# Seven block products in place of eight for the first layer's pooled gate, on a renormalised input, in a two-layer trunk

## The chip, the cores and the metric

The kernel runs on one core of a Trainium2 chip. The metric is the time of one execution in microseconds of the device, taken as the median of several runs. Five engines work in parallel, each through its own queue of instructions: TensorE (PE, matmuls; PEld is its loading of weights), VectorE (DVE), ScalarE (ACT), GpSimd (POOL) and SyncE (SP, which here only issues DMAs). DMAs are issued by SP, ACT and POOL.

## The reference, cut to what matters

A residual stream of T = 528 tokens (16 meta tokens and 512 others) by 1024 passes through two layers. Each layer is

```python
h = rmsnorm(h_res, norm_gain[l])
proj = h @ w_in[l]
u_pool, z_pool, c_q, c_kv, k_rope, z_mla, g_pool, g_mla = jnp.split(proj, IN_SPLIT_POINTS, axis=-1)
y_pool = (pool_mix(u_pool, ...) * jax.nn.silu(z_pool)) @ pool_w_up[l]
o_mla = mla(c_q, c_kv, k_rope, pos, ...)          # 8 heads, causal, rotary
y_mla = (o_mla * jax.nn.silu(z_mla)) @ mla_w_up[l]
merged = jax.nn.sigmoid(g_pool) * y_pool + jax.nn.sigmoid(g_mla) * y_mla
h_res = h_res + merged @ w_out[l]
```

and the output is the stream without the meta tokens. `g_pool` and `g_mla` are 1024 wide each: `h` (528 x 1024) times a 1024 x 1024 block of `w_in`. All is float32.

## The kernel before, in words

The stream lies transposed in SBUF: 8 row blocks of 128 features by the tokens (`xb`). A product in float32 is made of three: weights and input are each split into a high part in a shorter format and the rest (`split`, and `wload` for weights: ScalarE copies `hi`, VectorE subtracts to get `lo`), and `mm3` (L188, L191, L192) multiplies hi by hi, hi by lo and lo by hi into one PSUM bank. Weights come from DRAM in pieces of 128 x 512 (256 KB), three buffers deep, split as they come, four pieces ahead.

Nearly all matrix products of a layer stand in one list, `plan` (made by `register`, in the order in which it adds them: ckv, cq, u, k, v, zp, y, the queries qr and qn, pu, zm, the gates gp and gm, mu, o). `stream` walks through it. The rest of the program draws from the stream: `upto(name)` runs it up to a product, `fill_now(ns)` for so many nanoseconds of planned products. A planned product of three matmuls counts 3 n/2.4 ns for n columns, and `clk` is the sum of what has been drawn; it is a planner's clock, not the chip's. `after(ns, fn)` puts a step on the list until `clk` has grown by so much. The final order on each engine is set by a scheduler within these bounds.

In the attention of a layer (`head`, `pv`) the eight heads' own matmuls alternate with gaps (`gap`, four for each head), which draw the gates' products from the stream: `FILL` nanoseconds of them each, 2950 in the first layer and 2700 in the second, up to gm5 (`RESERVE`). A head's chain is: scores on TensorE, the maximum with the mask on VectorE (L886), the exponential on ScalarE (L893), scaling by the inverse sum on POOL (L900), transposes on TensorE (L957), a split, and the product with the values (L962, L963).

The two layers form their gates differently. In the first layer the input is x times the gain, not yet divided by the norm (`split_h`), all 528 tokens, in two halves of 264 columns. `ev_gp`, `ev_gm` and the `ev_silu` of zm multiply each result by the inverse norm `self.inv` (L716, L1038, L553) on VectorE; then comes Tanh on ScalarE. In the second layer (`self.last`) only 512 tokens are computed, and at the end of `qk_stats` the input is normalised and split anew (`renorm`, L576; row blocks 0 to 3 are fetched from DRAM as `xb` has been overwritten there). The gate gp of two neighbouring output tiles is a product of a 2 x 2 block of weights with a 2 x 2 block of input (two halves of K, two halves of the tokens); `fast` forms its four results from seven block products in place of eight, with sums of weights and of inputs. The input's sums and differences are made by `mixed` in the gaps (eight calls, four subtractions and three splits alternating), the weights' sums by DMA alone: `weight_sums` copies one block from DRAM to DRAM by SP (L350) and adds another to it by POOL (L353), eight transfers for each pair of tiles. Each is held behind a matmul that lies 14 us (copy) or 4 us (addition) back in planned time. The gates gm0 to gm5 of the second layer are stored in DRAM by ACT (L1047), from the slots `tc` and `ts` of the rotary tables, and fetched again before mu (`gates_again`). The last four columns of `wout` use the same seven products in both layers (`out_pairs`, `blend`).

## Time and profile before

| what | value |
|---|---|
| time, median of 3 runs | 782.66 us (782.34 to 786.49) |
| the profiled execution's own time | 781.06 us |
| its span | 779.3 us |
| granted TensorE clock | 1.0 throughout |
| TensorE busy | 772.7 us, 5469 matmuls |
| VectorE, ScalarE, POOL busy | 570.4, 445.9, 232.1 us |
| read from DRAM, written | 100.18 MB, 22.62 MB |
| first layer's attention | about 180 to 340 us |
| second layer's attention | about 580 to 700 us |

The profile is of one execution. Busy times overlap between engines. A matmul's own duration holds its way through the array and overlaps the next one's; the distance between the starts of two is what one costs. In the rows, "a<-b,c" is what an instruction writes and reads by the program's names, `L184` a line of the kernel, which can be that of a helper, and the number behind the bar the busy time, the mean of one in nanoseconds, then the idle time of the engine ahead of it and what ended it. In the rows of one tile or line, three numbers with slashes are the shortest, the median and the longest duration in nanoseconds. Rows that end in "x139, 256.0 KB, 3.0" are DMA issues with the median microseconds to landing.

### The profile page before, as it was taken

The numbers are of one execution on the slowest core, as the hardware profiler recorded it, in microseconds if no ns is written. First come the engines' busy times: TensorE is split into PE (matmuls) and PEld (weight loads), VectorE is DVE, ScalarE is ACT, GpSimd is POOL, SyncE is SP. The second block draws the span as 40 slices with busy tenths as digits, with TensorE's granted clock in tenths as the row PEclk, the third lists the DMA queues.
The fourth block names the chain that finished last, engine by engine and source line by source line (L and its number), as shares of the span: only waits on it lengthen the run. The fifth ranks groups of instructions, "written<-read, shape, count | busy, mean of one in ns | idle before, by whom it ended". The sixth has DMA issues, their size and how long they took to land.

```text
span 779.3 us, 15360 instructions
## 1 busy us (share of the span) xinstructions
PE 772.7 (99%) x5469; PEld 711.3 (91%) x5469; DVE 570.4 (73%) x1332; ACT 445.9 (57%) x1022; POOL 232.1 (30%) x303
## 2 busy tenths in 40 slices
PE   8999999999999999999999999999999999999998
PEld 8999899999999999999998898888788999988887
DVE  5848787546778876589764577865897888874984
ACT  7645655645566665645564346556657766664552
POOL 1024514103335333211330136112006625440213
PEclk9999999999999999999999999999999999999999
DMA  6243457765746465565662523435557666662655
GB/s 245 82 96 89 114 170 159 181 170 144 156 109 165 116 140 120 156 166 176 169 172 82 100 85 101 133 97 175 137 132 168 172 184 161 176 208 90 204 155 143
DMA packets 66189, 112.92 MB, mean 145 GB/s; under 512 B 10800, under 2 KB 16816, under 8 KB 66112
## 3 DMA queue, kind: packets, MB, share of 16 engines
q1 hardware_dynamic: 56208, 92.18, 39.8%
q0 software_dynamic: 8896, 17.92, 12.7%
q10 hardware_dynamic: 1008, 1.84, 0.7%
q8 instruction: 43, 0.70, 0.4%
q14 instruction: 34, 0.28, 0.1%
HBM read 100.18 MB, written 22.62 MB: 158 GB/s over the span
## 4 chain that ended last, share of the span: by engine, by line
PE 90%; DMA 4%; DVE 3%; ACT 2%; issue 1%; POOL 1%; SPq 0%; ACTq 0%; DVEq 0%
PE mm L188 26%; PE mm L192 25%; PE mm L191 25%; DMA raw<-win 2%; PE S L191 2%; PE S L192 2%; PE S L188 2%; PE mm L957 2%; PE o L963 1%; PE o L962 1%; PE S L500 1%; DVE wlo L184 1%; ACT whi L183 1%; DMA raw<-wqb 1%; PE mm L402 1%
## 5 line engine op out<-in xcount | busy, mean ns | idle before, releaser
L188 PE MATMUL mm<-hh,whi 128*128 128x264 f32 (+2 forms) x992 | 306.5, 311 | 0.9 <-ACT whi L183 0.8
L192 PE MATMUL mm<-hh,wlo 128*128 128x264 f32 (+2 forms) x992 | 304.2, 309 | 0.1
L191 PE MATMUL mm<-hl,whi 128*128 128x264 f32 (+2 forms) x992 | 304.1, 308 | 0.0
L184 DVE TENSOR_TENSOR wlo<-raw,whi 128x512 fp32r<-128x512 f32 (+2 forms) x261 | 182.5, 703 | 104.6 <-ACT whi L183 100.5
L183 ACT ACTIVATE whi<-raw 128x512 fp32r<-128x512 f32 (+2 forms) x261 | 156.6, 603 | 175.1 <-PE mm L191 106.6
L188 PEld LDWEIGHTS mm<-hh,whi 128*128 128x128 f32 x992 | 186.2, 188 | 11.9 <-ACT whi L183 1.1
L191 PEld LDWEIGHTS mm<-hl,whi 128*128 128x128 f32 x992 | 186.8, 188 | 8.8
L192 PEld LDWEIGHTS mm<-hh,wlo 128*128 128x128 f32 x992 | 185.8, 188 | 9.0 <-DVE wlo L184 0.7
L900 POOL TENSOR_SCALAR pa<-pa,rs 128x272 f32<-128x272 f32 (+1 forms) x32 | 33.2, 1036 | 103.3 <-DVE rs L919 63.9
L900 POOL TENSOR_SCALAR cq<-cq,rs 128x400 f32<-128x400 f32 (+1 forms) x32 | 51.1, 1597 | 0.0
L188 PE MATMUL mm<-cq,whi 128*128 128x264 f32 (+2 forms) x140 | 44.0, 314 | 0.6 <-ACT tmp L702 0.6
L191 PE MATMUL mm<-cq,whi 128*128 128x264 f32 (+2 forms) x140 | 43.5, 312 | 0.0
L192 PE MATMUL mm<-cq,wlo 128*128 128x264 f32 (+2 forms) x140 | 43.4, 312 | 0.0
L886 DVE CUSTOM_DVE_ANT_0 S<-S,maskw,nqs 128x272 f32<-128x272 f32 (+4 forms) x80 | 38.6, 498 | 5.3 <-PE S L192 5.0
L703 POOL TENSOR_TENSOR racc<-racc,tmp 128x264 f32<-128x264 f32 (+1 forms) x15 | 14.2, 949 | 87.2 <-ACT tmp L702 87.1
L298 DVE TENSOR_TENSOR tl<-mm,th 128x512 fp32r<-128x512 f32 (+1 forms) x64 | 30.0, 483 | 8.0 <-ACT th L297 6.3
L188 PE MATMUL mm<-u,whi 128*128 128x264 f32 (+1 forms) x108 | 35.2, 326 | 0.0
L192 PE MATMUL mm<-u,wlo 128*128 128x264 f32 (+1 forms) x108 | 34.8, 322 | 0.0
L353 POOL DMA_DIRECT2D wsum<-wout x8 | 7.0, 873 | 91.8 <-PE mm L192 87.1
L297 ACT ACTIVATE th<-mm 128x512 fp32r<-128x512 f32 (+1 forms) x64 | 26.2, 433 | 10.3 <-PE mm L957 9.8
L893 ACT ACTIVATE cq<-S,bia 128x400 f32<-128x400 f32 (+2 forms) x48 | 24.4, 513 | 13.2 <-DVE bia L931 8.5
L191 PE MATMUL mm<-kn,whi 128*128 128x264 f32 (+1 forms) x96 | 30.6, 320 | 0.0
(334 smaller groups left out, 1672.6 us busy)
## 6 DMA issues: line engine op xcount, KB each, us to landing
raw<-win SPq DMA_DIRECT2D x139, 256.0 KB, 3.0
raw<-wout SPq DMA_DIRECT2D x22, 256.0 KB, 3.6
bc<-kdr SPq DMA_DIRECT2D x16, 264.0 KB, 4.8
wsum<-wout SPq DMA_DIRECT2D x16, 256.0 KB, 4.0
raw<-wpu SPq DMA_DIRECT2D x16, 256.0 KB, 3.2
wsumgp<-win SPq DMA_DIRECT2D x16, 256.0 KB, 3.4
raw<-wmu SPq DMA_DIRECT2D x16, 256.0 KB, 2.6
raw<-wsumgp SPq DMA_DIRECT2D x16, 256.0 KB, 3.6
```

Source lines behind the costliest of these rows:

```text
L183: act.activation(hi[:, :n], raw[:, :n], AF.Copy)
L184: dve.tensor_sub(lo[:, :n], raw[:, :n], hi[:, :n].bitcast(F32))
L188: first = pe.matmul(out, wh, xh, start=start, stop=False, skip_group_check=more)
L191: pe.matmul(out, wh, xl, start=False, stop=False, skip_group_check=more)
L192: newest[0] = pe.matmul(out, wl, xh, start=False, stop=stop, skip_group_check=more)
L297: act.activation(hi[:, a:b], src, AF.Copy)
L298: dve.tensor_sub(lo[:, a:b], src, hi[:, a:b].bitcast(F32))
L703: self.acc_last = gp.tensor_add(self.acc[:, a:b], self.acc[:, a:b], t[:, :b - a])
L886: dve.tensor_tensor_reduce(out=sv, in0=sv, in1=mask, scale=nqs[:, i, h:h + 1], scalar=3e38, op0=ALU.add, op1=ALU.min, accum_out=bia[:, c:c ...
L893: act.activation(pv, sv, AF.Exp, scale=-1.0, bias=bia[:, i:i + 1], accum_out=rs[:, c:c + 1])
L900: gp.tensor_scalar(pt[i], pt[i], rs[:, i:i + 1], None, op0=ALU.mult)
L957: pe.transpose(tr[:, P * (i - j):P * (i - j + 1)], pt[i][:, NM + P * j:NM + P * (j + 1)], ident)
```

## The change

The first layer's path for the gates becomes that of the second. At the end of `qk_stats` both layers normalise and split the input anew; in the first layer blocks 0 to 3 are fetched from the kernel's input and the tokens are all 528, halves of 264. `ev_gp` and `ev_gm` go, `ev_zm` and `ev_gate` serve both layers, and gp is made by `fast` in both, its four pairs placed between the gm tiles. The constant halves of the tokens become `self.halves()`. Since gm uses the slots of the rotary tables, these are stored to DRAM after they are made (`kept`, by POOL) and fetched at the start of the second layer (`tables_again`, by SP). There are now sums of weights for gp of both layers: those for gp of the first, for `wout` of the first and for three of the four pairs of the second are started from the end of ckv1, one transfer every 3300 ns of planned time (`SUMS`), before 3850 from `k_factors` on; the fourth pair and `wout` of the second follow in the second layer, also every 3300 in place of 4500. `FILL` of the first layer is 2800.

```diff
-FILL = (2950.0, 2700.0)
+FILL = (2800.0, 2700.0)
+SUMS = 3300.0
...
+        for d, t in zip(kept, tab):
+            gp.dma_start(d, t)
+
+    def tables_again():
+        tab[:] = slot("tc")[:, :T], slot("ts")[:, :T]
+        for d, t in zip(kept, tab):
+            sp.dma_start(t, d)
...
-    wsum = {... for n, k in (("gp", 4), (0, 2), (1, 2))}
-    gate = dp.tile([P, 6, SEQ], F32, name="gate")
+    wsum = {... for n, k in (("gp0", 4), ("gp1", 4), (0, 2), (1, 2))}
+    gate = [dp.tile([P, 6, T], F32, name=f"gate{l}") for l in range(DEPTH)]
...
         def renorm(self, k):
-            f, (hh, hl), x = f[:, NM:T], self.hs[k], xb[:, k, NM:T]
+            x0 = self.x0
+            f, (hh, hl), x = f[:, x0:T], self.hs[k], xb[:, k, x0:T]
             if k < 4:
-                sp.dma_start(f, scr[:, k, :])
+                sp.dma_start(f, scr[:, k, :] if self.last else xT[:, k, :])
...
         def mixed(self, i):
-            if k > 3 or not self.last:
+            if k > 3:
                 return
+            a, b, c = self.halves()
+            n = b - a
...
-            if self.last:
-                start = clk[0]
-                for i, k in enumerate((4, 5, 6, 7, 0, 1, 2, 3)):
-                    self.renorm(k)
-                    fill_to(start + 1500 * (i + 1))
-            else:
-                fill_now(9500)
+            start = clk[0]
+            for i, k in enumerate((4, 5, 6, 7, 0, 1, 2, 3)):
+                self.renorm(k)
+                fill_to(start + 1500 * (i + 1))
...
         def ev_gate(self, m):
             def ev(ps, a, b):
-                self.gms[m] = slot(f"cq{m}" if m > 5 else "ts" if m % 2 else "tc")
+                if a == self.x0:
+                    self.gms[m] = slot(f"cq{m}" if m > 5 else "ts" if m % 2 else "tc")
                 act.activation(self.gms[m][:, a:b], ps, AF.Tanh, scale=0.5)
                 if m < 6:
-                    act.dma_start(gate[:, m, :], self.gms[m][:, a:b])
+                    act.dma_start(gate[self.l][:, m, a:b], self.gms[m][:, a:b])
...
-            if self.last:
-                for e in ("gm0", "gm1", "gp0", "gm2", "gp1", "gm3", "gp2", "gm4", "gp3", "gm5", "gm6", "gm7"):
...
-            else:
-                for m in range(8):
-                    add(f"gp{m}", wi(MT_GP + m), D, evac=self.ev_gp(m), xs=hs, segs=XS)
-                for m in range(8):
-                    add(f"gm{m}", wi(MT_GM + m), D, evac=self.ev_gm(m), xs=hs, segs=XS)
+            for e in ("gm0", "gm1", "gp0", "gm2", "gp1", "gm3", "gp2", "gm4", "gp3", "gm5", "gm6", "gm7"):
+                m = int(e[2])
+                if e[:2] == "gp":
+                    self.fast(e, wi(MT_GP + 2 * m), wi(MT_GP + 2 * m + 1), m, self.got_gp)
+                else:
+                    add(e, wi(MT_GM + m), D, evac=self.ev_gate(m), xs=hs, segs=XS)
...
         def go(self, nxt):
             up("ckv1")
...
+            if l == 0:
+                wg = [[win[l_, MT_GP + m] for m in range(8)] for l_ in range(DEPTH)]
+                sums = [*weight_sums("gp0", wg[0]), *weight_sums(0, [wout[0, m] for m in OUT]),
+                        *weight_sums("gp1", wg[1], range(3))]
+                for i, fn in enumerate(sums):
+                    after(SUMS * (i + 1), fn)
+            else:
+                tables_again()
...
-            if l == 0:
-                sums = [*weight_sums(0, [wout[0, m] for m in OUT]), *weight_sums("gp", [win[1, MT_GP + m] for m in range(8)])]
-                for i, fn in enumerate(sums):
-                    after(3850 * (i + 1), fn)
...
-            if l == 0:
-                fill_now(2600)
             kq = self.prep(0)
             if l == 1:
-                for i, fn in enumerate(weight_sums(1, [wout[1, m] for m in OUT])):
-                    after(4500 * (i + 1), fn)
+                sums = [*weight_sums("gp1", [win[1, MT_GP + m] for m in range(8)], (3,)),
+                        *weight_sums(1, [wout[1, m] for m in OUT])]
+                for i, fn in enumerate(sums):
+                    after(SUMS * (i + 1), fn)
...
-            if self.last:
-                self.gates_again()
+            self.gates_again()
```

More of the change, by code (lines that the diff above doesn't have):

```diff
@@ L353, in add @@
             behind(gp.dma_start(d, src[1], accum_op=ALU.add), earlier(4000))
-        for u in range(len(w) // 2):
+        for u in units or range(len(w) // 2):
             for fn, i in ((copy, 0), (copy, 2), (add, 0), (copy, 1), (add, 2), (add, 1), (copy, 3), (add, 3)):
@@ L571, in renorm @@
             f = self.f[k] = slot("sv", bufs=2) if k % 4 == 3 else slot(f"cq{k}")
[L572 removed]
+            x0 = self.x0
+            f, (hh, hl), x = f[:, x0:T], self.hs[k], xb[:, k, x0:T]
             if k < 4:
[L574 removed]
+                sp.dma_start(f, scr[:, k, :] if self.last else xT[:, k, :])
                 x = f
[L576 removed]
+            behind(dve.scalar_tensor_tensor(out=f, in0=x, scalar=self.g(G_H + k), in1=self.inv[:, x0:T],
                                             op0=ALU.mult, op1=ALU.mult), newest[0])
[L578 removed]
+            split(hh, hl, f, x0, T)
         def mixed(self, i):
             k, s = divmod(i, 2)
[L582 removed]
+            if k > 3:
                 return
+            a, b, c = self.halves()
+            n = b - a
             u, w = self.f[k], self.f[k + 4]
@@ L595, in mixed @@
             th, tl = (slot(f"cq{(3, 0, 1, 2)[k] + j}", F32R) for j in (0, 4))
-            t3h, t3l, t4h, t4l = (t[:, :N2] for t in self.half[4 * k:4 * k + 4])
+            t3h, t3l, t4h, t4l = (t[:, :n] for t in self.half[4 * k:4 * k + 4])
             split(th, tl, u[:, a:c], a, c)
             for h_, l_, v in ((t3h, t3l, w[:, b:c]), (t4h, t4l, w[:, a:b])):
-                split(h_, l_, v, 0, N2)
+                split(h_, l_, v, 0, n)
             self.tt[k] = {6: (th[:, a:b], tl[:, a:b]), 5: (th[:, b:c], tl[:, b:c]), 7: (t3h, t3l), 4: (t4h, t4l)}
@@ L603, in fast @@
             order = (1, 6, 7, 5, 2, 4, 3)
-            s = wsum["gp"][u]
+            s = wsum[f"gp{self.l}"][u]
+            lo, mid, hi = self.halves()
+            n = mid - lo
+            A, B = (lo, mid), (mid, hi)
             src = {1: a[:, 0:512], 2: a[:, 512:1024], 4: b[:, 512:1024], 5: s[:, 0, :], 6: s[:, 1, :], 7: s[:, 2, :],
@@ L710, in ev @@
                 act.activation(self.am[m][:, a:b], ps, AF.Copy)
-            return ev
-        def ev_gp(self, m):
-            def ev(ps, a, b):
-                t = tmp()
-                dve.tensor_mul(t[:, :b - a], ps, self.inv[:, a:b])
-                act.activation(t[:, :b - a], t[:, :b - a], AF.Tanh, scale=0.5)
-                dve.scalar_tensor_tensor(out=self.am[m][:, a:b], in0=t[:, :b - a], scalar=1.0,
-                                         in1=self.am[m][:, a:b], op0=ALU.add, op1=ALU.mult)
             return ev
@@ L1052, in gates_again @@
                 self.gms[m] = slot(f"cq{m}")
-                sp.dma_start(self.gms[m][:, NM:T], gate[:, m, :])
+                sp.dma_start(self.gms[m][:, self.x0:T], gate[self.l][:, m, self.x0:T])
         def ev_mu(self, m):
@@ L1330, in go @@
             up("gm6")
-            if self.last:
-                self.gates_again()
+            self.gates_again()
             up("gm7")
```

63 lines of the change are left out of this document (23 added, 40 removed).

## The prediction

> **What bounds the kernel now.** I read the page first (engine shares and the chain that ended last), then stretches of the span by engine, then single rows.
>
> ```profile
> span 779.3 us, 15360 instructions
> PE 772.7 (99%) x5469; PEld 711.3 (91%) x5469; DVE 570.4 (73%) x1332; ACT 445.9 (57%) x1022; POOL 232.1 (30%) x303
> ...
> PE 90%; DMA 4%; DVE 3%; ACT 2%; issue 1%; POOL 1%; SPq 0%; ACTq 0%; DVEq 0%
> ```
>
> TensorE is busy 99% of the span and makes 90% of the chain. So a matmul taken out is worth its own time, as long as the engines that feed it keep ahead. The stretches show whether they do; columns are stretch, length, then busy time of each engine, clock, DMA share.
>
> ```profile
> core 0: us, PE busy (x) PEld busy (x) DVE busy (x) ACT busy (x) POOL busy (x), PEclk, DMA share, GB/s
> 20.00:92.00 72.00, 72.00 (x606) 67.02 (x605) 51.44 (x118) 39.05 (x88) 25.12 (x26) 1.00 0.34 95
> 92.00:127.00 35.00, 34.38 (x277) 33.99 (x276) 25.82 (x70) 18.53 (x41) 6.96 (x13) 1.00 0.62 157
> 127.00:180.00 53.00, 53.00 (x446) 51.31 (x445) 29.80 (x69) 29.79 (x74) 11.50 (x14) 1.00 0.68 168
> 180.00:340.00 160.00, 160.00 (x1300) 158.16 (x1299) 118.37 (x318) 93.53 (x243) 58.09 (x79) 1.00 0.58 140
> 550.00:580.00 30.00, 30.00 (x138) 24.25 (x138) 29.05 (x70) 19.75 (x39) 0.89 (x1) 1.00 0.44 118
> 580.00:700.00 120.00, 119.55 (x782) 108.49 (x781) 100.62 (x264) 81.26 (x213) 57.99 (x71) 1.00 0.67 182
> 155.00:180.00 25.00, 25.00 (x215) 23.68 (x208) 11.11 (x35) 11.06 (x27) 1.65 (x2) 1.00 0.64 160
> ```
>
> The attention of the first layer, with its gates in the gaps, is 180 to 340; that of the second, where seven products are already in use, is 580 to 700. The second is the model for what the first becomes: there TensorE idles 120 - 119.55 = 0.45 us, with VectorE busy 100.62/120 = 84% and ScalarE 81.26/120 = 68%. The first has 74% and 58% and no idle TensorE. The renormalising of the second layer lies in 550 to 580, that of the first would come into 155 to 180.
>
> **The products removed.** Eight gate tiles take 8 x 2 halves x 8 blocks of K x 3 = 384 matmuls of 264 columns. Seven products for each of four pairs take 4 x 7 x 4 x 3 = 336. So 48 fall away. Their price is the distance between starts, as a single matmul's duration overlaps the next one's:
>
> ```profile
> 127.75 0.28 PE L191 MATMUL mm<-cq,whi 128*128 128x264 f32 x1
> ...
> 137.99 0.28 PE L191 MATMUL mm<-cq,whi 128*128 128x264 f32 x1
> ```
>
> Those are the first and the last of 85 rows in a row, all of 264 columns: (137.99 - 127.75)/84 = 0.122 us. 48 x 0.122 = **-5.85 us**, all of it on the path.
>
> **The vector work of the gates.** These rows price it.
>
> ```profile
> L716 DVE TENSOR_TENSOR tmp<-mm,rinv 128x264 f32<-128x264 f32 x16 | 6.8, 428 | 3.2 <-PE mm L192 3.1
> L1038 DVE TENSOR_TENSOR cq<-mm,rinv 128x264 f32<-128x264 f32 x16 | 6.9, 430 | 6.2 <-PE mm L192 6.0
> L553 DVE SCALAR_TENSOR_TENSOR u<-mm,rinv 128x264 f32<-128x264 f32 x8 | 3.4, 431 | 0.7 <-PE mm L192 0.6
> L184 DVE TENSOR_TENSOR wlo<-raw,whi 128x512 fp32r<-128x512 f32 x233 | 168.5, 725 | 95.7 <-ACT whi L183 93.8
> L298 DVE TENSOR_TENSOR hl<-cq,hh 128x528 fp32r<-128x528 f32 x8 | 5.6, 702 | 0.0
> L298 DVE TENSOR_TENSOR u<-cq,cq 128x264 fp32r<-128x264 f32 x8 | 3.2, 426 | 0.0
> L183 ACT ACTIVATE whi<-raw 128x512 fp32r<-128x512 f32 x233 | 146.1, 630 | 164.6 <-PE mm L191 104.2 <-DMA raw<-win 24.2 <-issue 8.6
> L297 ACT ACTIVATE hh<-cq 128x528 fp32r<-128x528 f32 x8 | 5.1, 640 | 4.3 <-DVE cq L1063 4.3
> L297 ACT ACTIVATE cq<-cq 128x264 fp32r<-128x264 f32 x8 | 3.0, 415 | 0.2
> ```
>
> Away go the multiplications by the inverse norm at the gates and at zm: 16 x 0.428 + 16 x 0.430 + 8 x 0.431 = 17.2 us of VectorE. Added in `mixed` are 16 subtractions of a half (0.43), and for each of four k one split of a full row and two of a half: VectorE 16 x 0.43 + 4 x (0.70 + 2 x 0.43) = 13.1, ScalarE 4 x (0.64 + 2 x 0.42) = 5.9. `fast` adds five combinations of a half for each pair, 20 x 0.43 = 8.6 of VectorE, and four copies on ScalarE (1.7). The weights come in 4 x 7 = 28 pieces in place of 16, since each piece now feeds 12 matmuls, not 24: 12 more splits, VectorE 12 x 0.725 = 8.7, ScalarE 12 x 0.63 = 7.6. Net VectorE 13.1 + 8.6 + 8.7 - 17.2 = +13.2, ScalarE +15.2. In a stretch of 160 - 5.85 = 154 us VectorE comes to 131.6/154 = 85%, ScalarE to 108.7/154 = 71%: the level of the second layer. Taking that layer's idle rate, 0.45 x 154/120 = **+0.6 us**. The bounds are -0.3 (shorter eviction of zm and the gates) and +3.4 (eight `mixed` calls each keeping TensorE back 0.42 us, one half-row operation).
>
> The gates gm keep their Tanh, their storing to DRAM moves 12 issues onto ScalarE's queue, and the reload of six rows waits on SyncE for the `cq` rows of the last pair, with the mu weights behind it. Between that pair and the first use lie two gate tiles, 96 matmuls x 0.122 = 11.7 us, and mu0. I take 0; without that cover the price is one landing.
>
> **Renormalising.** It replaces 9.5 us of filler by eight steps of 1.5 us, and the 2.6 us before the first head go, so the first head comes at the same point (12.1 against 12.0 us of planned products).
>
> ```profile
> L576 DVE SCALAR_TENSOR_TENSOR cq<-xb,gn,rinv x3: 729/750/753, 549.0 to 553.3; 128x512 f32<-128x512 f32 x3
> ...
> L576 DVE SCALAR_TENSOR_TENSOR sv<-sv,gn,rinv x1: 733/733/733, 563.6 to 563.6; 128x512 f32<-128x512 f32 x1
> 178.44 0.28 PE L188 MATMUL mm<-hh,whi 128*128 128x264 f32 x1
> ```
>
> The cost is 8 x (0.75 x 528/512 + 0.70) = 11.8 us of VectorE and 8 x 0.64 = 5.1 of ScalarE, into a stretch (155 to 180) where VectorE has 13.9 and ScalarE 13.9 us free. The second layer needs from 549.0 to about 565, 16 us. Here from 156 that ends near 172, and the first product that reads the new input, zm0, starts at 178.44. The pu products (192 x 0.122 = 23.4 us) hide it: **0**. Were VectorE 10 us later, TensorE would wait some 4 us.
>
> **Sums of weights.** There are 96 transfers in place of 64, half of them copies on SyncE, half additions that POOL issues; 72 of them belong to the first layer, one every 3.3 us of planned products from the end of ckv1 (2.6 us ahead of the sums of the norm, L402 at 24.26, so about 21 us), in place of 48 from 91 us, one every 3.85.
>
> ```profile
> L353 POOL DMA_DIRECT2D wsum<-wout x8: 812/860/1046, 110.7 to 648.2; - x8
> L353 POOL DMA_DIRECT2D wsumgp<-wsumgp x8: 833/884/897, 198.8 to 344.8; - x8
> L350 SPq DMA_DIRECT2D wsum<-wout x16: 496/519/1087, 91.3 to 647.1; - x16
> 24.26 2.36 PE mm L402 x40
> raw<-win SPq DMA_DIRECT2D x139, 256.0 KB, 3.0
> 106.53 4.88 DMA raw<-win
> PE mm L188 <- ACT tmp L702: 0.6, 1, 0.6
> PE mm L957 <- POOL pa L900: 0.2, 1, 0.2
> 586.96 0.82 POOL L353 DMA_DIRECT2D wsum<-wout  x1 [8.83 <-PE mm L192]
> 587.56 1.40 POOL L900 TENSOR_SCALAR pa<-pa,rs 128x272 f32<-128x272 f32 x1
> L900 POOL TENSOR_SCALAR pa<-pa,rs x32: 632/960/2813, 180.7 to 689.4; 128x272 f32<-128x272 f32 x16, 128x144 f32<-128x144 f32 x16
> ```
>
> The first 20 to 92 us ran at a DMA share of 0.34 and will run near 0.6. The nearest rows are the three stretches at 0.58 to 0.68: 0.62 us of idle TensorE in 35 + 53 + 160 = 248 us, all of it at 126, where a weight piece took 4.88 us to land against a median of 3.0. At that rate 72 us cost 0.2, and at the rate of 92 to 127 alone 1.3. Below nothing: the wait at 126 may vanish (-0.6), since the order of transfers there changes. I take **+0.3**. Behind the copies on SyncE queue weight pieces; behind the additions on POOL queue the sums of squares, the rotary products, the window sums and, in the attention, the softmax scaling. The row at 586.96 shows the last: an addition ahead of a scaling, and TensorE waits 0.2 us. In the second layer's attention 12 additions replace 8: **+0.1**, at most 4 x 0.9 = 3.6 if each cost its whole issue. The Trainium skill, page "SBUF — State Buffer", section "SBUF: two separate sides" (its warning box on POOL's DMAs, with figures in the section after it), says the reverse of this cheapness: descriptors of POOL's DMAs can't be written while certain VectorE operations hold the shared port, so that a transfer of 0.62 us alone took 3.1 us. Here the longest issue is 1.05 us while VectorE is 74 to 84% busy, so no such lock shows in the issues; it keeps a small chance below.
>
> All first-layer sums end near 72 x 3.3 = 238 us of planned products after 21 us, about where the last one ends now (345 us); the pairs' own sums, first in the list, are 32 x 3.3 = 106 us in, well ahead of the first pair. The rotary tables' store and reload and the small edits at meta queries: 0, in queues with nothing urgent behind. FILL falls by 0.15 us in each of 32 gaps, 4.8 us, against 48 x 0.11 = 5.3 us of planned products less: the filler lasts as long as before.
>
> **Sum.** -5.85 + 0.6 + 0.3 + 0.1 = -4.85 us. The profiled run took 781.06 us (span 779.3 and 1.8 around it); 776.2 after. The median of the runs, 782.66, is 1.6 us above it, so **777.8**. 0.5% of the median, about what a measurement of this kernel tells from no change, is 3.9 us: faster means under 778.75.
>
> **Rivals.** First, half is given back: weight pieces arrive late in the first 130 us, each time as at 126. Five more such waits of 0.62 cost 3.1 us: 780.9. For it: VectorE and ScalarE have little room at 92 to 127 (74% and 53%) and three pieces in a row arrive late there. Against: 127 to 180 has the highest DMA share and no idle time. Chance 0.17.
>
> Second, slower: the first layer's head chain gets behind VectorE's new queue. Eight times a `mixed` call puts 1.6 to 1.7 us of work (four subtractions, or three splits) before a head's maximum, and TensorE waits for it. All eight cost 8 x 1.6 = 12.8, 790.6; with six it is 787.4; it decides from three on (4.85/1.6), where nothing is left. Against: the second layer makes the same eight calls and idles 0.45 us altogether. For: this layer's gap is shorter than before and has the meta queries as well. Chance 0.11.
>
> Third, slower, by POOL's queue: additions hold POOL and the softmax scaling behind them is late by as much as the longest scaling row lies over the median, 2.81 - 0.96 = 1.85 us. Some seven more additions fall into attention (18.7 in place of 16 in the first layer, 12 in place of 8 in the second): 7 x 1.85 = 13.0, less 4.85, gives 790.8; from three on nothing is left. It is the case by the port rule above; the issues of 0.8 to 1.05 us speak against. Chance 0.04.
>
> That fewer products aren't what comes out (the stream runs dry before the last head and TensorE waits there) would give about 782.7; filler and gaps shrink alike. Chance 0.03.
>
> **Numbers.** The forecast has 0.65 and covers 776.2 to 778.7. Faster than that by losing the wait at 126 and a quiet run (0.3 below the median): 775.8, the low end. The high end takes in the first rival and no gain at all: 783.0; beyond lie the second and third. Faster by over 0.5%: 0.65 + 0.02 of the first rival = 0.67; within 0.5%: 0.15 + 0.03 = 0.18; slower: 0.15.
>
> **What would show it.** TensorE's count falls by 48 to about 5421 and its busy time by 5 to 6 us; 180 to 335 has VectorE at 84 to 86% and TensorE idle under 1 us; zm0 starts near 178 with no wait for `hl`; the stretch 20 to 92 has a DMA share near 0.6 and TensorE busy over 99%. I am wrong if TensorE waits on ScalarE's `whi` or VectorE's `wlo` before 130 us (first rival), on VectorE's bias or `hl` between 155 and 340 (second), on POOL's `pa` (third).

## The result

The changed kernel takes 804.26 us (median of 6 runs, 798.37 to 806.32) against 782.8 before: a ratio of 1.0262, 95% interval 1.0238 to 1.0286. It is slower by 2.6%, where I had forecast 0.6% faster.

First the page of the kernel after, the same lines as shown of before.

```profile
span 803.9 us, 15499 instructions
...
PE 779.4 (97%) x5421; PEld 714.3 (89%) x5421; DVE 587.5 (73%) x1368; ACT 460.3 (57%) x1058; POOL 246.9 (31%) x321
...
PE 84%; DMA 6%; DVE 5%; ACT 2%; issue 1%; POOL 0%; SPq 0%; ACTq 0%; DVEq 0%; POOLq 0%
```

The 48 matmuls are gone (5469 to 5421). TensorE's idle time has grown from 779.3 - 772.7 = 6.6 to 803.9 - 779.4 = 24.5 us, and its busy time has grown by 6.7 although it has less to do. DMA has gone from 4% to 6% of the chain, VectorE from 3% to 5%. TensorE's waits, longest first (who waited for whom, us in total, times, longest):

```profile
PE mm L189 <- ACT whi L184: 7.0, 3, 4.0
PE o L962 <- ACT th L298: 4.7, 1, 4.7
PE S L189 <- ACT sv L1131: 2.3, 1, 2.3
PE mm L957 <- POOL pa L900: 1.9, 2, 1.7
```

The first is a weight piece that isn't there. The second looks like attention's own work on ScalarE; ScalarE's order of time ahead of it shows what it is:

```profile
323.99 0.63 ACT L298 ACTIVATE q<-tmp 128x512 fp32r<-128x512 f32 x1
330.11 0.63 ACT L184 ACTIVATE whi<-raw 128x512 fp32r<-128x512 f32 x1 [5.49 <-DMA raw<-win]
330.64 0.58 ACT L298 ACTIVATE th<-mm 128x512 fp32r<-128x512 f32 x1
```

ScalarE stands 5.49 us before the split of a weight piece that hasn't landed, and attention's split `th` is queued behind it. The chain of work has that piece; after the start in us stands its time from issue to landing:

```profile
321.12 8.89 DMA raw<-win
```

That is 8.89 us against the median of 3.0 before. SyncE's order of time around it shows what it shares the engines with:

```profile
320.11 0.90 SPq L1043 DMA_DIRECT2D cq<-gate  x2
321.12 0.37 SPq L116 DMA_DIRECT2D raw<-win  x1
321.53 1.39 SPq L1043 DMA_DIRECT2D cq<-gate  x3
```

The piece is issued between five rows of stored gates, 264 KB each, which the change makes the first layer fetch again, and one addition of a sum is issued by POOL at 320.79. So the longest wait has the reload beside it and not the sums alone. More on this stands below, with the runs that leave sums out.

The wait at 60 us came in another way. Its chain holds a store of the inverse norms (`ndr`), and only then the weight piece:

```profile
41.58 10.68 DMA ndr<-ny
...
53.24 6.58 DMA raw<-wkb
```

SyncE may fetch the norms only when their store has landed, and stands before the two fetches for 8.1 us, in the kernel before for 7.8; the weight pieces are queued behind them in both. What differs is the landing of the piece: 6.58 us, against a median of 2.0 for the pieces of `wkb` before, and it meets a stream that has just run short.

Each long wait has an aftermath. In these short stretches the last three columns are the granted clock, the DMA share and GB/s:

```profile
core 0: us, PE busy (x) PEld busy (x) DVE busy (x) ACT busy (x) POOL busy (x), PEclk, DMA share, GB/s
56.00:60.00 4.00, 1.82 (x15) 1.61 (x13) 0.00 (x0) 0.07 (x1) 0.00 (x0) 1.00 1.05 299
60.00:63.00 3.00, 2.50 (x11) 2.06 (x12) 1.59 (x3) 2.14 (x5) 0.75 (x1) 0.74 0.72 249
63.00:66.00 3.00, 2.81 (x14) 2.53 (x13) 2.42 (x7) 0.74 (x3) 2.69 (x3) 0.50 0.35 95
66.00:70.00 4.00, 4.00 (x26) 4.00 (x26) 2.36 (x6) 2.39 (x5) 0.13 (x1) 0.72 0.86 149
122.00:126.00 4.00, 0.91 (x5) 0.70 (x6) 1.00 (x3) 1.67 (x5) 0.00 (x0) 1.00 0.49 162
126.00:130.00 4.00, 4.00 (x21) 4.00 (x22) 3.13 (x9) 1.47 (x4) 0.00 (x0) 0.57 0.46 144
212.00:216.00 4.00, 2.33 (x17) 2.12 (x16) 3.69 (x16) 2.68 (x8) 1.96 (x2) 0.88 0.84 246
216.00:220.00 4.00, 4.00 (x26) 4.00 (x25) 0.56 (x2) 1.32 (x7) 4.00 (x7) 0.70 0.18 41
324.00:330.00 6.00, 2.60 (x23) 2.37 (x21) 2.54 (x8) 0.62 (x2) 0.00 (x0) 1.00 0.98 251
330.00:334.00 4.00, 2.72 (x11) 2.63 (x12) 2.84 (x8) 3.89 (x12) 0.00 (x0) 0.63 0.84 310
334.00:338.00 4.00, 4.00 (x32) 3.96 (x31) 0.79 (x2) 0.53 (x3) 3.23 (x4) 0.94 0.38 119
```

TensorE runs dry at 56 to 60, 122 to 126, 212 to 216 and 324 to 330 us, and behind each of them it gets a lower clock: in 126 to 130 it is "busy" for all 4 us and makes 21 matmuls, where 4/0.122 = 33 fit. A mean of 0.74 over 3 us is 2 x 0.26 x 3 = 1.6 us at half clock; all eight rows with less than 1.00 give 1.6 + 3.0 + 2.2 + 3.4 + 1.0 + 2.4 + 3.0 + 0.5 = 17.1 us at half clock, or 8.5 us of work lost on top of the waits. The kernel before had a clock of 1.0 throughout. The Trainium skill ("TensorE: Matmul & The Clock Gate", Part 1) describes a clock that falls to half after an idle window of about 3.4 us and stays there for such a window. These rows agree on the stay, with about 3.4 us at half clock after three of the waits and 6.8 after the one at 60. They differ on the fall: a wait of 2.6 us at 60, and waits of 1.7 and 0.7 near 213, were enough here.

So the added span of 24.6 us is 17.9 of idle time and 6.7 of busy time. Of the latter -5.85 for the matmuls and +8.5 for the clock make 2.65; some 4 us are not placed. Where the loss lies:

```profile
20.00:130.00 110.00, 103.04 (x809) 96.51 (x808) 70.69 (x175) 53.34 (x119) 37.76 (x48) 0.95 0.65 152
200.00:345.00 145.00, 135.08 (x1061) 131.51 (x1060) 107.97 (x288) 89.09 (x233) 60.58 (x78) 0.98 0.68 180
```

That is 7.0 us of idle time and 5.1 of lost clock before 130 us, and 9.9 and 3.4 in the first layer's attention. So about half is lost ahead of the first gate: the first sum of weights is loaded as a piece at 224.51 us, and up to 130 us every piece feeds as many matmuls as it did before. The mean DMA share of 0.65 hides stretches in which the engines are full, 1.05 at 56 to 60 and 0.98 at 324 to 330; being full alone makes no wait, for the kernel before has 1.04 at 146 to 148 and loses nothing there.

### The profile page after: what moved, and what is told of

Read it like the earlier page. It is cut to its first block, busy times and chain, and to the rows that moved or that the text cites. A ratio compares the mean times of both kernels' runs of the same rounds, so it can differ in the third digit from the quotient of the medians.

```text
span 803.9 us, 15499 instructions
## 1 busy us (share of the span) xinstructions
PE 779.4 (97%) x5421; PEld 714.3 (89%) x5421; DVE 587.5 (73%) x1368; ACT 460.3 (57%) x1058; POOL 246.9 (31%) x321
## 3 DMA queue, kind: packets, MB, share of 16 engines
q1 hardware_dynamic: 61968, 102.77, 41.9%
q0 software_dynamic: 11360, 22.66, 15.9%
## 4 chain that ended last, share of the span: by engine, by line
PE 84%; DMA 6%; DVE 5%; ACT 2%; issue 1%; POOL 0%; SPq 0%; ACTq 0%; DVEq 0%; POOLq 0%
PE mm L189 24%; PE mm L193 23%; PE mm L192 23%; DMA raw<-win 3%; PE S L189 2%; PE S L193 2%; PE S L192 2%; PE mm L957 2%; DMA ndr<-ny 1%; DVE wlo L185 1%; PE o L963 1%; PE o L962 1%; ACT whi L184 1%; PE S L506 1%; DMA raw<-wkb 1%
## 5 line engine op out<-in xcount | busy, mean ns | idle before, releaser
L189 PE MATMUL mm<-hh,whi 128*128 128x264 f32 (+2 forms) x912 | 286.4, 317 | 6.1 <-ACT whi L184 4.4
L192 PE MATMUL mm<-hl,whi 128*128 128x264 f32 (+2 forms) x912 | 284.5, 313 | 0.0
L193 PE MATMUL mm<-hh,wlo 128*128 128x264 f32 (+2 forms) x912 | 283.8, 314 | 0.2 <-DVE wlo L185 0.2
L189 PEld LDWEIGHTS mm<-hh,whi 128*128 128x128 f32 x912 | 174.6, 192 | 18.3 <-ACT whi L184 5.2
L192 PEld LDWEIGHTS mm<-hl,whi 128*128 128x128 f32 x912 | 174.9, 192 | 8.9
L193 PEld LDWEIGHTS mm<-hh,wlo 128*128 128x128 f32 x912 | 174.0, 192 | 9.1 <-DVE wlo L185 0.8
L189 PE MATMUL mm<-cq,whi 128*128 128x264 f32 (+2 forms) x172 | 53.2, 309 | 0.0
L192 PE MATMUL mm<-cq,whi 128*128 128x264 f32 (+2 forms) x172 | 52.5, 306 | 0.0
L359 POOL DMA_DIRECT2D wsumgp<-win x16 | 13.9, 869 | 94.2 <-PE mm L193 49.6
L886 DVE CUSTOM_DVE_ANT_0 S<-S,maskw,nqs 128x288 f32<-128x288 f32 (+4 forms) x80 | 38.3, 497 | 5.9 <-PE S L193 5.6
L192 PEld LDWEIGHTS mm<-cq,whi 128*128 128x128 f32 x172 | 32.4, 188 | 1.7
L189 PEld LDWEIGHTS mm<-cq,whi 128*128 128x128 f32 x172 | 32.4, 188 | 1.7
```

Source lines behind the costliest of these rows:

```text
L189: first = pe.matmul(out, wh, xh, start=start, stop=False, skip_group_check=more)
L192: pe.matmul(out, wh, xl, start=False, stop=False, skip_group_check=more)
L193: newest[0] = pe.matmul(out, wl, xh, start=False, stop=stop, skip_group_check=more)
L359: behind(gp.dma_start(d, src[1], accum_op=ALU.add), earlier(4000))
L886: dve.tensor_tensor_reduce(out=sv, in0=sv, in1=mask, scale=nqs[:, i, h:h + 1], scalar=3e38, op0=ALU.add, op1=ALU.min, accum_out=bia[:, c:c ...
```

## The experiments

All ratios are to the kernel before on the same chip. Theory A: the transfers for sums make weight pieces late. Theory B: the new vector work does.

**Without the sums' transfers.**

```diff
-        for u in units or range(len(w) // 2):
+        for u in ():
```

(and the four sums replaced by plain blocks as the source of the loads)

> The kernel after, without any of the 96 transfers that make the sums of weights; the seven products load plain blocks of the same size in place of the sums (so the numbers it computes are not the reference's). Theory A, the traffic of the sums makes weight pieces late and TensorE's clock halves after each long wait: 776 to 781 us, granted clock 0.999 or more, no wait of TensorE over 1 us after the start. Theory B, the vector work of renorm, mixed and fast holds TensorE up: 795 us or more, with the waits still there between 155 and 340 us. A mixture lies between, and says how much is left for gates and tables.

782.24 us, ratio 0.9996 (0.998 to 1.0012). Taking the transfers out brings 804.26 - 782.24 = 22.0 us, all that the kernel after had lost. But the gain of 5.85 isn't there either, and two waits remain, at 198 and 202 us, with a half-clock window behind them. The control, with the 64 transfers taken out of the kernel before:

> Control: the kernel before, without its 64 transfers for sums (plain blocks in their place, so other numbers). The traces of before show two waits only, so all theories expect 781 to 783 us; if it is faster by more than 2 us, the sums had a price in the kernel before as well, and the comparison of no sums with before has to be made against this one.

780.18 us, 0.9971 (0.9956 to 0.9986). The sums cost 2.0 us before and 22.0 after. Without sums the change is 2.1 us slower, not 5.85 faster: 7.9 us are lost elsewhere.

**When the transfers start.** The kernel after with its 72 first-layer transfers started at `k_factors`, and the kernel before with its own 48 started early:

```diff
+LATE = 2600.0
...
             self.k_factors()
+            if l == 0:
+                ...
+                for i, fn in enumerate(sums):
+                    after(LATE * (i + 1), fn)
```

> The kernel after, with the first layer's 72 transfers for sums started at k_factors as before (about 91 us), one every 2.6 us of planned products, so that they end about as in the kernel after. Theory A1, the early start is the harm (waits at 60 and 125 us): those two waits and their half-clock windows go, about 12 us less, 790 to 794. Theory A2, it is the amount of traffic wherever it falls: 800 to 810, the waits move to 100 to 340. Theory B: within 3 us of the kernel after.

804.05 us, 1.0276 (1.0234 to 1.0318).

> The kernel before, with its own 48 transfers for sums started at the end of ckv1, one every 3.3 us, and nothing else changed. Theory A1, the early start is the harm: 790 to 796 us, with long waits near 60 and 125 us. Theory B: 781 to 784, as before.

792.7 us, 1.0143 (1.0114 to 1.0172), with waits at 73 and 126 us. Its stretch up to 130 us, with the gates of before and nothing of the change but the early start:

```profile
20.00:130.00 110.00, 101.39 (x801) 94.40 (x800) 68.90 (x174) 52.47 (x118) 36.87 (x46) 0.97 0.63 146
```

So 48 transfers placed early cost 10 us, with 8.6 us of idle time before 130 us, and 72 pressed into the later part cost as much as 72 spread from the start. Theory A holds for either place in the first layer.

**Which transfers, and which queue.**

```diff
-            behind(sp.dma_start(d, src[0]), earlier(14000))
+            behind(act.dma_start(d, src[0]), earlier(14000))
```

> The kernel after, with the 48 copies issued by ScalarE's queue in place of SyncE's; the traffic is the same. If weight pieces are late because they stand behind copies in SyncE's own queue: 785 to 793 us. If they are late because the 16 engines are shared by all that is in flight: 798 to 808. Under theory B: slower than the kernel after by the 48 issues of 0.33 us on ScalarE at most, 804 to 820.

800.81 us, 1.0246 (1.022 to 1.0272), against 1.0262 (1.0238 to 1.0286) with the copies on SyncE: the two intervals overlap. So the copies' place in SyncE's queue is a small part of the loss at most.

```diff
-            behind(gp.dma_start(d, src[1], accum_op=ALU.add), earlier(4000))
+            pass
```

> The kernel after without the 48 additions that POOL issues (so the sums are plain blocks and the numbers differ); the 48 copies stay as they are. If the two halves of the traffic do equal harm: 791 to 795. If the additions do most, as they read twice and take 5.6 us to land against 3.9: 784 to 789. If the copies do, because they stand in SyncE's queue ahead of weight pieces: 798 to 803.

783.28 us, 1.0011 (0.9995 to 1.0027): better than any of the forecasts. Without the 48 additions 21 of the 22 us of harm are gone, and the 48 copies of the same bytes that are left cost 1. The additions without the copies were not run, and neither was a plain copy issued by POOL; so it is open how much of the 21 us needs both, and whether it comes from the adding or from POOL's kind of queue (q0 below). Queue rows (packets, MB, share of 16 engines) of after, of the copies alone, and of no sums:

```profile
q1 hardware_dynamic: 61968, 102.77, 41.9%
q0 software_dynamic: 11360, 22.66, 15.9%
```

```profile
q1 hardware_dynamic: 61968, 102.77, 44.2%
q0 software_dynamic: 4448, 10.07, 4.6%
```

```profile
q1 hardware_dynamic: 55056, 90.18, 38.4%
```

(q0 of no sums is as with the copies alone.) The additions are 22.66 - 10.07 = 12.59 MB and take 0.159 x 803.9 - 0.046 x 780.6 = 92 us of all 16 engines; the copies, 102.77 - 90.18 = 12.59 MB as well, take 0.442 x 780.6 - 0.384 x 780.3 = 45 us. An addition occupies the engines twice as long as a copy, 1.9 us against 0.95. A share of busy time doesn't show what that does to others; the landing of weight pieces between 40 and 135 us (shortest, median, longest) does, again after, copies alone, no sums:

```profile
DMA to landing us min/median/max: 2.0/3.6/9.2
```

```profile
DMA to landing us min/median/max: 1.7/2.7/6.9
```

```profile
DMA to landing us min/median/max: 1.7/2.6/4.9
```

The piece between the gates' rows, 8.89 us in the kernel after, lands in 4.63 with the copies alone and 4.30 with no sums; the rows themselves land in 4.2 us without sums and 9.1 with them (medians). So the reload alone makes no long wait. No run takes the reload away and leaves the sums, so its part in the 4.7 us is open.

**The vector work.** Where the loss without sums comes from is in VectorE's order of time. Before, the Newton steps that give the heads' scale `nqs` and the first maximum (L886):

```profile
161.45 0.18 DVE L305 TENSOR_SCALAR ny<-na 128x40 int32<-128x40 int32 x1
...
164.95 0.18 DVE L828 TENSOR_SCALAR nqs<-ny 128x40 f32<-128x40 f32 x1
...
177.18 0.51 DVE L886 CUSTOM_DVE_ANT_0 S<-S,maskw,nqs 128x272 f32<-128x272 f32 x1 [1.67 <-PE S L192]
```

The kernel without sums:

```profile
162.33 0.18 DVE L306 TENSOR_SCALAR ny<-na 128x40 int32<-128x40 int32 x1
...
169.19 0.42 DVE L595 TENSOR_TENSOR cq<-cq,cq 128x264 f32<-128x264 f32 x1
...
183.49 0.17 DVE L830 TENSOR_SCALAR nqs<-ny 128x40 f32<-128x40 f32 x1
...
186.79 0.49 DVE L885 CUSTOM_DVE_ANT_0 S<-S,maskw,nqs 128x272 f32<-128x272 f32 x1
```

The same small steps take 3.5 us in the one and 21 in the other: renorm's 0.75 us operations stand between them, and so do the subtractions and splits of `mixed` (L595 and on), which the program places in the gaps of the heads but the scheduler has moved up. VectorE is busy without a break and the first head's chain is about 10 us late. Theory C, then: this burst. Each call of `mixed` is held behind the newest matmul at its place:

```diff
-                dve.tensor_sub(w[:, b:c], u[:, b:c], w[:, b:c])
+                behind(dve.tensor_sub(w[:, b:c], u[:, b:c], w[:, b:c]), newest[0])
...
-            split(th, tl, u[:, a:c], a, c)
+            split(th, tl, u[:, a:c], a, c, newest[0])
```

(`split` puts the ScalarE copy behind it; the two half splits likewise)

> The kernel without transfers for sums (plain blocks in their place, so other numbers), and in addition each call of mixed is held behind the newest matmul at its place, so that its subtractions and splits can't be moved up next to renorm, ahead of the Newton steps and the first maxima. Theory C, this burst on VectorE between 160 and 200 us is what still eats the saving of 5.85 us: TensorE's waits at 198 and 202 us and the half-clock window behind them go, 776 to 779 us. Rival D, the vector work as such (eviction, weights in 28 pieces) does: within 1.5 us of the kernel without sums, 781 to 784.

782.23 us, 1.0001 (0.9984 to 1.0018): no change in the sum, yet the waits at 198 and 202 us are gone. In their place TensorE waits at 610, in the second layer, whose `mixed` I had held too. With the sums in:

> The kernel after with mixed held in the gaps and the sums as they are. Theory C: the waits near 211 and 215 us and their half-clock window go, 4 to 6 us less than after, 797 to 801. Rival D: 802 to 806.

803.65 us, 1.0261 (1.0236 to 1.0286), the same pattern. Held in the first layer alone:

> The kernel without transfers for sums (plain blocks, other numbers), with mixed held in its gaps in the first layer only; the second layer's is free to move up again, since holding it there had brought a wait near 610 us. Theory C in this form, each hoisted burst of VectorE work costs only where it meets the first heads: both waits gone, 777 to 780 us, against 782.2 with neither held. If holding has no net worth: 781.5 to 784.

778.65 us, 0.9949 (0.9929 to 0.9969). `nqs` is ready again at

```profile
174.25 0.18 DVE L835 TENSOR_SCALAR nqs<-ny 128x40 f32<-128x40 f32 x1
...
175.72 0.51 DVE L890 CUSTOM_DVE_ANT_0 S<-S,maskw,nqs 128x272 f32<-128x272 f32 x1 [1.29 <-PE S L193]
```

and now VectorE waits for the scores, as before. Theory C is shown, at 3.6 us, for the first layer; in the second the early burst does no harm and holding it does.

**Spreading the sums over both layers.** 48 transfers in each, started at that layer's `k_factors` and made for that layer's gp and `wout`, `mixed` held in both:

```diff
             self.k_factors()
+            sums = [*weight_sums(f"gp{l}", ...), *weight_sums(l, ...)]
+            for i, fn in enumerate(sums):
+                after((3850, 3300)[l] * (i + 1), fn)
```

> The kernel after with mixed held, and the same 96 transfers laid out in another way: 48 in each layer, started at that layer's k_factors (first layer every 3.85 us of planned products as in before, second every 3.3), the sums of a layer's gp and wout in that layer. If the harm comes from where and how densely the first layer's 72 transfers lie: 776 to 782, no half-clock window before 340 us. If it is the total traffic: 790 or more, with waits moved into the second layer's attention (580 to 700).

789.78 us, 1.0092 (1.0056 to 1.0128): 14 us better than after with `mixed` held, between the forecasts. No half-clock window is left before the end, but short waits remain in both layers' attention; at the head of four of them stands a weight piece that took 3.9 to 5.6 us to land.

**One more buffer for weight pieces** (paid for by one of the three buffers of the keys' factors, whose fetch then has to follow a use):

```diff
-        return wp.tile([P, 512], F32, tag="raw", name=nm("raw"), bufs=3)
+        return wp.tile([P, 512], F32, tag="raw", name=nm("raw"), bufs=4)
...
-        self.bcs[h] = bc = slot("bc", bufs=3)
+        self.bcs[h] = bc = slot("bc", bufs=2)
...
-            if h + 2 < H:
-                self.spread_k(h + 2)
             dve.tensor_mul(kf, self.kn[p] if odd else self.kp, bc)
+            if h + 2 < H:
+                self.spread_k(h + 2)
```

> The kernel after with four buffers for weight pieces as they land in place of three, paid for by two in place of three buffers for the keys' norm factors (their fetch is issued after the use of the one before). Nothing else changes, all 96 transfers and their times stay. Theory E, the pieces of seven products feed 12 matmuls of 0.122 us, 1.5 us in place of 2.9, so that three buffers cover too little of a slow landing: 790 to 797, the waits at 60, 125 and 330 us shortened by 1.5 to 3 us each and half-clock windows fewer. If it is bandwidth alone, a buffer more changes nothing: 802 to 806. If the keys' factors come late: waits of VectorE on bc in every head, over 806.

784.64 us, 1.0032 (1.0014 to 1.0051): 19.6 us less than after, with the same 96 transfers, and with weight pieces that land no sooner (again between 40 and 135 us):

```profile
DMA to landing us min/median/max: 2.1/4.3/9.3
```

The control has the other half of the edit alone, two factors' buffers with the later fetch:

> Control for the fourth weight buffer: the kernel after with only the other half of that edit, two in place of three buffers for the keys' factors with their fetch behind the use of the one before; three weight buffers as in after. If the fourth buffer is what gave 19.6 us: 802 to 807, as after. If it was the later fetch of the factors (fewer transfers ahead of weight pieces at 105 to 117 us): 785 to 795.

798.9 us, 1.0197 (1.0162 to 1.0233). The later fetch makes some 5 of the 19.6 us, the fourth buffer the other 14. The pieces are as late as ever; with a buffer more they can be asked for sooner. The buffer works mainly in the first layer's attention: from the control to the kernel with the buffer, TensorE's idle time goes from 5.0 to 3.9 us in 20 to 130, and from 10.1 to 4.4 us in 200 to 345. There stands `fast`, in which a piece feeds 12 matmuls, 12 x 0.122 = 1.5 us, where a piece of a plain gate feeds 24, 2.9 us. The change halves there, in microseconds, the way that a given number of pieces looks ahead, and makes the landing longer (median 3.8 us in 200 to 345, 2.6 without sums). That the halving is why the buffer helps so much is argued: no run changes what a piece feeds and keeps the transfers. For the loss before 130 us it is no explanation, and theory E was wrong to count the waits at 60 and 125 us as its own; the piece at 60 is one of `wkb`, 128 KB, and feeds 12 matmuls in both kernels.

The same edit in the kernel before, and its control:

> The kernel before with four weight buffers and two for the keys' factors, nothing else. Its pieces feed 24 matmuls in the first layer's gates and its trace shows two waits of 0.6 and 0.2 us, so lookahead has little to give: 780.5 to 782.5. If it falls to 778 or less, the buffer is a gain of its own and the change, with the sums spread, has none beside it.

> The kernel before with two buffers for the keys' factors and the later fetch, three raw buffers: the half of the deeper-buffer edit that is not the buffer. If the fourth raw buffer is what brought the kernel before from 782.8 to 777.4 us, this stays at 782 to 783. If the later fetch moves the wait at 126 us, it comes to 778 to 780. After the change this half was worth 5.4 us of 19.6; scaled to 5.4 that would be 1.5, 781.3, which I take.

777.44 us, 0.9936 (0.9919 to 0.9953), and 782.19, 0.9997 (0.9983 to 1.0012): there the buffer makes all of it. TensorE's waits of the kernel before, with the buffer, are down to one of 1.0 us at the start.

**All repairs together.** The changed kernel with the buffer and `mixed` held in the first layer, its sums as in the change, and then with its sums spread over both layers:

> The kernel after with four weight buffers and mixed held in the first layer; sums placed as in after. Against 784.6 with the buffer alone, holding takes the waits at 204 and 208 us and their half-clock window: 779 to 782. If 777 to 779, spreading the sums over both layers is worth nothing once the buffer is there; if 783 or more, holding is worth nothing.

> All of it together: the sums spread over both layers (48 transfers each from k_factors on), mixed held in the first layer, four buffers for weight pieces. From 789.8 us (spread, mixed held in both layers) the free second layer takes 2 to 3 us and the fourth buffer 3 to 5: 781 to 785 under theories C and E. Under 780 it beats the kernel before; at 787 or more, neither holds here.

780.49 us, 0.9978 (0.9957 to 0.9999), and 777.81, 0.9942 (0.9927 to 0.9957). That beats the kernel before, but not the kernel before with the same buffer (777.44): the two can't be told apart, and I know of no faster version that computes everything. Where the 48 matmuls' worth stayed is in two stretches, first of the kernel before with the buffer, then of the repaired change:

```profile
0.00:20.00 20.00, 18.67 (x125) 17.50 (x126) 10.73 (x21) 15.71 (x28) 2.97 (x13) 1.00 0.72 252
200.00:345.00 145.00, 145.00 (x1181) 143.54 (x1180) 109.76 (x290) 85.22 (x220) 49.65 (x67) 1.00 0.58 143
```

```profile
0.00:20.00 20.00, 17.22 (x114) 16.38 (x115) 9.78 (x19) 14.61 (x26) 2.97 (x13) 1.00 0.73 252
200.00:345.00 145.00, 142.28 (x1129) 138.61 (x1128) 115.60 (x302) 92.24 (x242) 52.75 (x70) 0.99 0.70 186
```

The repaired change idles 1.45 us more at the start, where neither kernel differs by intent, and 2.7 us in the first layer's attention, where DMA share and VectorE are higher.

**Is the gain there at all?** Both kernels with the buffer and without sums, the changed one with `mixed` held in the first layer:

> The kernel before without its 64 transfers for sums (plain blocks stand in for the sums) and with four raw buffers. Without sums there is little to wait for: 780.18 us with three buffers, of which the profile gave 5.4 us idle. If the buffer's worth is relief from late pieces alone, 778 to 780; if it is worth 5.4 us of its own here too, 775.

> The changed kernel without sums, mixed held in the first layer, four raw buffers: every cost that was found is taken away. If the 48 matmuls are worth their 5.85 us once nothing is late, this is 5 to 6 us under the kernel before without sums and with four buffers, some 773 us. If the change has a cost of its own that is still unfound (28 pieces for 16, VectorE at 85%), the gap stays at the 1.5 us seen with three buffers, some 777 us. I take 774.

776.41 us, 0.992 (0.9905 to 0.9936), against 773.8, 0.9884 (0.9861 to 0.9906). The gain exists: 2.6 us, in the profiles' spans 776.2 - 772.5 = 3.7. It is about half of 5.85. The pages' lines:

```profile
PE 771.2 (99%) x5469; PEld 712.0 (92%) x5469; DVE 570.6 (74%) x1332; ACT 445.9 (57%) x1022; POOL 205.8 (27%) x271
```

```profile
PE 766.5 (99%) x5421; PEld 705.6 (91%) x5421; DVE 589.4 (76%) x1368; ACT 459.7 (60%) x1058; POOL 210.2 (27%) x273
```

TensorE's busy time falls by 4.7, and idle time grows from 5.0 to 6.0. All of that and more is in the stretch 200 to 345, of the changed kernel

```profile
200.00:345.00 145.00, 143.60 (x1158) 140.55 (x1157) 119.16 (x309) 93.62 (x244) 41.86 (x59) 1.00 0.49 149
```

with 1.4 us of idle time, where its counterpart has none:

```profile
200.00:345.00 145.00, 145.00 (x1180) 143.50 (x1179) 109.76 (x291) 85.35 (x220) 38.34 (x54) 1.00 0.32 97
```

The list of waits places 1.2 of the 1.4 us near 250 us: 0.9 on ScalarE's copy to `racc` and 0.3 on its split `th`, at the end of some 5 us in which ScalarE works without a break, two weight splits and the Tanh of a gate among it. With the sums spread over both layers the changed kernel is 777.81 - 773.8 = 4.0 us slower, the kernel before with its own sums 777.44 - 776.41 = 1.0. The difference of 3 us takes up the 2.6.

| median us | three buffers | four buffers |
|---|---|---|
| before | 782.8 | 777.44 |
| before, no sums | 780.18 | 776.41 |
| after | 804.26 | 784.64 |
| after, `mixed` held in the first layer | not run | 780.49 |
| the same, sums spread | not run | 777.81 |
| the same, no sums | 778.65 | 773.8 |

## Why the prediction was wrong

Forecast 777.8, measured 804.26, outside the range of 775.8 to 783.0 and on the other side.

**Products removed, -5.85.** 48 fewer, as said. On the path they are worth 2.6 to 3.7 us even where everything found has been repaired and the sums are away. TensorE's busy time falls by 4.7; the rest goes into idle time in the first layer's attention.

**Sums of weights, +0.3 and +0.1.** This is the step that failed. It measured 22.0 us in the changed kernel against 2.0 before: +20. I took idle time per microsecond from stretches with a DMA share of 0.58 to 0.68 and applied it to 20 to 92 us. The share was forecast well (0.65 between 20 and 130), but it isn't what decides: the kernel before has the same 0.65 between 130 and 200 and loses nothing there, and loses 8.6 us at 0.63 between 20 and 130 once its own sums start early. At 60 us the pieces stand behind the norms' fetch in SyncE's queue, in both kernels, so that a slow landing meets a stream that is already short; I priced that at the rate of other stretches. In the first layer's attention I counted 28 pieces for 16 as 12 more splits on VectorE and ScalarE, and not as a halved lookahead. I also priced each wait as its length alone, 0.62 us, and misread the row for it: the piece ahead of the wait at 126 is the third of the three late ones, `wqb` with 5.46 us, and not the one of 4.88. The waits came at up to 4.7 us, with 8.5 us of lost clock behind them. And I took a copy and an addition for the same transfer; the addition holds the engines twice as long, and with the additions gone 21 of the 22 us are gone.

**Reload of the gates, 0.** It was weighed for the mu weights behind it. In the kernel after it stands around the late piece of the longest wait; its own price was not measured.

**First rival.** It named the place and the sign, weight pieces late before 130 us with TensorE waiting on `whi`; its size, five waits of 0.62, was a quarter of the 12 us lost there, and it stopped at 130 us, where a late piece hits attention too: it holds `th` behind `whi` on ScalarE, at 324 to 330 us. I had weighed what is queued behind the transfers on SyncE and POOL, and not what is queued behind a split that waits for one.

**Renormalising, 0, and vector work of the gates, +0.6.** I found 11.8 us of VectorE for 155 to 180 and 13.9 free, and let `mixed` follow in the gaps of the heads. The scheduler put it straight behind `renorm`, and the first head's maximum was late by some 10 us: 782.24 - 778.65 = 3.6 us. The order was to be read in the trace of before, in its second layer: the rows of the subtractions there are

```profile
L586 DVE TENSOR_TENSOR cq<-cq,cq x3: 405/405/407, 558.9 to 564.8; 128x256 f32<-128x256 f32 x3
L589 DVE TENSOR_TENSOR sv<-sv,sv x1: 406/406/406, 574.3 to 574.3; 128x256 f32<-128x256 f32 x1
```

and lie at 559 to 574, ahead of the attention at 580, and not in its gaps. The price that I gave ("Were VectorE 10 us later, TensorE would wait some 4 us") came close by luck: I had meant zm0's input, which was not waited for, as forecast. The waits came in the first heads, on the scaling (1.7 us) and the exponential (0.7), with a half-clock window behind them.

**Second and third rival.** The second had the right engine and consequence, but eight calls in eight gaps; it was one burst ahead of the first head. The third had the right culprit, the additions, by a mechanism that the rows don't bear out: POOL's issues of them stay short in the kernel after,

```profile
L359 POOL DMA_DIRECT2D wsumgp<-win x16 | 13.9, 869 | 94.2 <-PE mm L193 49.6 <-PE mm L192 44.6
```

as they were before (medians of 0.86 and 0.88), and TensorE's longest wait on `pa` is 1.7 us with the sums and without. What changes is the landing of the pieces beside them. The chance of 0.15 for slower was too small for a term whose nearest rows lay in other stretches, with other things in SyncE's queue.

**Open.** Some 4 us of TensorE's busy time in the kernel after; why an addition that is spread over 16 engines delays a piece by as much as it does (that it takes them for 1.9 us and not 0.95 is measured, the way from there to a landing of 9.2 us is not); whether the adding or POOL's queue is at fault; and what the gates' reload costs beside the sums. That the additions be made on an engine instead of by DMA was not tried.

## What to carry to other kernels

Measure the lookahead of a stream of weights in microseconds of matmuls, pieces ahead times what one piece feeds, and set it against the longest landing: a saving that halves what a piece feeds halves the lookahead, and one more buffer was worth 14 us here while a mean DMA share of 0.65 said nothing. Look also for fetches that wait for a store in the queue that issues the weights, as at 60 us. Price a wait of TensorE by its length and the half clock behind it, and add what stands behind the waiting split on its engine. Where a second place in the kernel already does what the change brings to the first, read there where the scheduler really put the work, not where the program calls it; and try a buffer on the kernel as it is first, for it gave 5 us without the change.

## What the runs showed of the hardware that I had not expected

An addition by DMA from DRAM to DRAM took the 16 engines 92/48 = 1.9 us for 256 KB, a copy of the same size 45/48 = 0.95; the additions were issued by POOL and the copies by SyncE, and no run separates the two. TensorE's waits of 4.0 and 4.7 us, and two of 1.7 and 0.7 close together near 213 us, were each followed by 3.4 us at half clock, one of 2.6 at 60 us by 6.8, in all 8.5 us of lost work in a span of 803.9. POOL's issues of additions took 0.83 to 0.87 us in the mean with VectorE at 73%, so they show nothing of the lock that the third rival rested on.
